# The first five microseconds of an encoder layer: early activation, ten matmuls on constants, and smaller first transfers

## The chip, the core and the metric

The kernel runs on one core of one Trainium2 chip. The metric is the device time of one execution in microseconds; lower is better. Of three runs of the kernel before, the median is 820.86 us (820.34 to 820.87). Engines are named as the profile does: PE is TensorE, DVE is VectorE, ACT is ScalarE, SP is the engine that issues most transfers; PEld are PE's weight loads. A name with q behind it (SPq, ACTq) is the queue of transfers that the engine issues.

## The reference

One layer of a bidirectional encoder trunk on 256 tokens of 1024 features, in fp32: a feed-forward half step, a mixer (latent attention beside a two-way state space scan), and a second half step. Only the beginning of the first half step matters here:

```python
def rmsnorm(x, g):
    y = xf * lax.rsqrt(jnp.mean(xf * xf, axis=-1, keepdims=True) + EPS)
    return (y * g).astype(x.dtype)

def swiglu(h, w_gate, w_up, w_down):
    return (jax.nn.silu(h @ w_gate) * (h @ w_up)) @ w_down

x = x + 0.5 * swiglu(rmsnorm(x, ffn1_norm[l]), ffn1_w_gate[l], ffn1_w_up[l], ffn1_w_down[l])
...
x = x + 0.5 * swiglu(rmsnorm(x, ffn2_norm[l]), ffn2_w_gate[l], ffn2_w_up[l], ffn2_w_down[l])
```

The hidden width of the half step is 2816, so w_gate and w_up are each 1024 x 2816.

## The kernel before

x lies transposed in SBUF, as 8 tiles (k = 0 to 7) of 128 features by 256 tokens. A half step goes through 22 blocks of 128 hidden features (f = 0 to 21). In each block PE forms the gate and the up product, [128 hidden x 256 tokens], over the 8 k tiles. To keep fp32 accuracy every operand is split in two parts of a narrower type, hi and lo: ACT writes the hi part by a copy (helper `copy`, L94) and DVE the lo part by a subtraction (helper `tt`, L97, for weights, `stt`, L100, for x). A product is then three matmuls (`mm3`, L136 to L138): hi times hi, hi weights times lo x, lo weights times hi x, the third needing the lo part of the weights. A block is therefore 2 x 8 x 3 = 48 matmuls.

A weight piece is fetched from HBM into a buffer called `raw` (4 buffers) and split into `whi` and `wlo` (4 buffers each); this is `wload`, L112. From f = 1 on a block has two pieces of 512 KB, gate and up. x is split by `Norm.scale` into `xh` and `xl` after a product with the gain, which lies in the constant tile `vec`; the sum of squares over features is collected in `nacc` (`Norm.square`), summed over features on PE (`ps_sum`, L181), turned into 1/sqrt on DVE, spread on PE (`ps_rows`, L190) and read as `R`. The products of a block leave PSUM only by a multiplication with `R`, so until `R` is there they wait in the six PSUM buffers of the tag `mm`.

In the first half step block 0 differs (L248 to L254): the weights come in four pieces of 256 KB (gate, first and second half, then up), and the eight `scale` stand between the first piece and the other three. x comes in three transfers (L166 to L168: tiles 0-1, 2-3, 4-7), the first from SP, the two others from ACT behind `vec`. PE does all 24 matmuls of gate and then all 24 of up.

Each engine runs its instructions in the order of the program; a scheduler of the language works this order out when the program is built, from priorities (`WPRI`, L31, puts the splitting of weights ahead of other work). DVE and ACT also have small work in this stretch that nothing waits for soon: rotary tables (`rp_...`), masks, and constants made from `cst` and `row`. Transfers report their end through eight counters, DMAHW0 to DMAHW7, which the program uses in turn; a transfer that gets a counter still in use by an earlier one waits in its issuing queue until that one has landed.

The name of a tile at a wait is that of the tile being written: `xh`, `xl`, `whi`, `wlo`, `ps_gu` (gate and up products).

Of the kernel before, what the change touches and what calls it, by code (L numbers as in the profile page):

```python
# [8 lines left out]
F32 = mybir.dt.float32  # L9
# [14 lines left out]
# pool depths  # L24
# [3 lines left out]
# blocks of the first half step during which the mixer's first weights are fetched  # L28
PREF = (8, 10, 12, 14, 16, 18)
# how far the splitting of weights runs ahead of other work  # L30
WPRI = 50  # L31
# emission order of the mixer, in rounds (one round per group of the state space part):
# attention units, state space units, its norm, weight chunks
# [15 lines left out]
# columns of the packed per-feature vectors  # L49
V_F1, V_MIX, V_F2, V_QA, V_KVA, V_SSM, V_DSK, V_CW, V_CB = 0, 8, 16, 24, 27, 29, 45, 61, 181  # L50
V_N = 205
# columns of the packed per-column rows
R_DTB, R_AL, R_GQ, R_GK, R_IF = 0, 64, 128, 224, 320
R_N = 336
# columns of the constant matrices
# [17 lines left out]
def build(ctx, tc, A, out, dbg=None):  # L73
# [66 lines left out]
    def wstat(ps, pieces, xh, xl, k0, first, last):  # L140
        """ps[feature, token] += sum over the k tiles held in pieces"""
        ks = [(pc, j) for pc, j0, n in pieces for j in range(j0, j0 + n)]
        for i, (pc, j) in enumerate(ks):
            mm3(ps, pc.hi[:, j * P:(j + 1) * P], pc.lo[:, j * P:(j + 1) * P],
                xh[:, k0 + i], xl[:, k0 + i], first and i == 0, last and i == len(ks) - 1)

    def rsqrt(y, v, n):
        """y = v ** -0.5 on [P, n]"""
        t = sm.tile([P, 8], I32, tag="rs_t", name="rs_t")[:, :n]
        a = sm.tile([P, 8], F32, tag="rs_a", name="rs_a")[:, :n]  # L150
        w = sm.tile([P, 8], F32, tag="rs_w", name="rs_w")[:, :n]
        ts(t, v.bitcast(I32), 1, None, ALU.logical_shift_right)
        ts(y.bitcast(I32), t, -1.0, float(0x5F3759DF), ALU.mult, ALU.add)
        ts(w, v, -0.5, None, ALU.mult)
        for _ in range(3):
            tt(a, y, y, ALU.mult)
            tt(a, a, w, ALU.mult)
            stt(y, a, 1.5, y, ALU.add, ALU.mult)

# [4 lines left out]
    x = xp.tile([P, KD, T], F32, name="x")  # L164
    nc.scalar.dma_start(vec, A["vec"])
    nc.sync.dma_start(x[:, 0:2], A["xt"][:, 0:2])  # L166
    nc.scalar.dma_start(x[:, 2:4], A["xt"][:, 2:4])
    nc.scalar.dma_start(x[:, 4:8], A["xt"][:, 4:8])  # L168
# [4 lines left out]
    V.memset(ones, 1.0)  # L173
    halfpi = cp.tile([P, 1], F32, name="halfpi")
    V.memset(halfpi, PI / 2)

    def token_sums(psp, sq, tag):
        """[token, 2]: the sum of sq[feature, token] over its features"""
        ps = psp.tile([P, 512], F32, tag=tag, name="ps_sum")
        for t in range(2):  # L180
            TE.matmul(ps[:, t:t + 1], sq[:, t * P:(t + 1) * P], ones[:, 0:1], start=True, stop=True)  # L181
        return ps[:, 0:2]

    def token_rows(psp, r, tag):
        """[P, token]: r[token, 2] on every partition"""
# [19 lines left out]
    class Norm:  # L205
        """x * gain of each tile of x as it comes, and the sum of squares"""
# [30 lines left out]
    def ffn(norm, wgu, wd, after, hook=None):  # L237
        with ExitStack() as es:
# [7 lines left out]
            for f in range(KF):  # L246
                ps = ps_mm.tile([P, 2, T], F32, tag="mm", name="ps_gu")
                if f == 0 and hook:  # L248
                    pcs = wload(wgu[f], [512], 0)
                    for k in range(KD):  # L250
                        norm.scale(k)
                    pcs += wload(wgu[f, :, 512:2048], [512] * 3, 0)
                    for j in range(2):
                        wstat(ps[:, j], [(pcs[2 * j], 0, 4), (pcs[2 * j + 1], 0, 4)], norm.xh, norm.xl, 0, True, True)  # L254
                else:
                    pcs = wload(wgu[f], [1024, 1024])
# [7 lines left out]
                tt(gu, ps, R.unsqueeze(1).to_broadcast([P, 2, T]), ALU.mult)  # L264
# [25 lines left out]
    def tables():  # L290
# [7 lines left out]
        # 0 where a pair of tokens counts, -2**100 elsewhere  # L298
# [67 lines left out]
    with ExitStack() as es:  # L366
# [63 lines left out]
        # rotated shared key and its square sum  # L430
# [12 lines left out]
        # dt = softplus(raw + bias), log-decay sums  # L443
# [22 lines left out]
        # log-decay sums counted from the middle of the sequence outwards  # L466
# [72 lines left out]
        def attn_group(g):  # L539
            st = {}  # L540

            def proj():
# [20 lines left out]
                # head norms  # L563
# [11 lines left out]
                # rotary part of q, in place  # L575
# [7 lines left out]
                # k  # L583
# [211 lines left out]
def _tiles(w):  # L795
    """[K, M] -> [M tiles, partition, K tiles, 128]"""
    k, m = w.shape
    return w.reshape(k // P, P, m // P, P).transpose(2, 1, 0, 3)


def _pairs(t):
    """[n, P, K, 128] -> [n / 2, P, 2 * K * 128]"""
# [89 lines left out]
```

## Time and profile before

| | before |
|---|---|
| median of 3 runs | 820.86 us (820.34 to 820.87) |
| profiled execution: span from first to last instruction | 817.6 us |
| PE busy | 797.8 us, 98% |
| DVE busy | 590.3 us, 72% |
| ACT busy | 470.2 us, 58% |
| read from HBM | 124.52 MB, 154 GB/s over the span |

Of the profiled execution the profile tells the span alone; the device time of a run has 3.3 us more than it (820.86 - 817.6), which lie ahead of the first instruction and behind the last. Times in rows are counted from the start of the span. A busy share of PE includes the waiting inside its pipeline, so the spacing of matmul starts says more of its pace than the share. The column PEclk reads 1.00 in all of this trace, also in the first 15 us.

### The profile page before, as it was taken

To read this page: it belongs to the slowest core of one execution; us is meant where nothing else is said; L and a number is where in the kernel's file an instruction comes from. 1 tells how busy PE (TensorE), PEld (TensorE's weight loads), DVE (VectorE), ACT (ScalarE), POOL (GpSimd) and SP (SyncE) were. 2 spreads that over 40 slices of the span, in tenths; PEclk is the share of its full clock that TensorE was granted. 3 is DMA by queue.
4 is the path that set the end of the run, shared out by engine and by line. 5 is a ranking of instruction groups with operands and counts; after the bars stand their busy time and mean duration, and the time that the engine had idled before them with its cause. 6 is when DMAs were issued, how large, how long until landed. Compare 5 with 4: busy or idle time off the path is not lost.

```text
span 817.6 us, 16082 instructions
## 1 busy us (share of the span) xinstructions
PE 797.8 (98%) x6480; PEld 768.8 (94%) x6480; DVE 590.3 (72%) x1192; ACT 470.2 (58%) x810; POOL 0.2 (0%) x4
## 2 busy tenths in 40 slices
PE   6999999999998999999999999999999999999998
PEld 5999999999998998988989999999999999999998
DVE  6977776566797986897897578657787766666543
ACT  6755554455367659679676666557455544444342
POOL 0000000000000000000000000000000000000000
PEclk9999999999999999999999999999999999999999
DMA  7667774667235443322325414342665555554772
GB/s 259 214 212 224 222 229 136 184 184 215 63 92 171 131 131 104 106 79 92 103 85 168 154 52 154 112 146 68 223 184 178 175 184 182 185 184 131 197 206 75
DMA packets 39098, 126.61 MB, mean 155 GB/s; under 512 B 4464, under 2 KB 5872, under 8 KB 39024
## 3 DMA queue, kind: packets, MB, share of 16 engines
q1 hardware_dynamic: 38592, 124.69, 48.7%
q8 instruction: 51, 0.84, 0.4%
q10 hardware_dynamic: 432, 0.89, 0.3%
q14 instruction: 23, 0.19, 0.1%
HBM read 124.52 MB, written 1.05 MB: 154 GB/s over the span
## 4 chain that ended last, share of the span: by engine, by line
PE 86%; DVE 6%; ACT 5%; DMA 2%; issue 1%; ACTq 0%
PE ps_gu L137 10%; PE ps_gu L138 10%; PE ps_gu L136 10%; PE ps_d L136 5%; PE ps_d L137 5%; PE ps_d L138 5%; PE ps_in L137 4%; PE ps_in L138 4%; PE ps_in L136 4%; PE ps_y L690 3%; PE ps_sb L138 2%; PE ps_sb L137 2%; PE ps_sb L136 2%; PE ps_sc L603 2%; PE ps_gt L137 1%; PE ps_o L630 1%
## 5 line engine op out<-in xcount | busy, mean ns | idle before, releaser
L94 ACT ACTIVATE whi<-raw 128x1024 fp32r<-128x1024 f32 (+4 forms) x256 | 251.3, 986 | 209.0 <-PE ps_d L137 53.1
L97 DVE TENSOR_TENSOR wlo<-raw,whi 128x1024 fp32r<-128x1024 f32 (+4 forms) x256 | 289.8, 1134 | 112.1 <-ACT whi L94 111.2
L136 PE MATMUL ps_gu<-xh,whi 128*128 128x256 f32 x704 | 201.0, 285 | 7.9 <-ACT whi L94 7.9
L137 PE MATMUL ps_gu<-xl,whi 128*128 128x256 f32 x704 | 201.2, 286 | 0.5 <-DVE xl L100 0.4
L138 PE MATMUL ps_gu<-xh,wlo 128*128 128x256 f32 x704 | 200.8, 285 | 0.0
L136 PEld LDWEIGHTS ps_gu<-xh,whi 128*128 128x128 f32 x704 | 136.5, 194 | 8.2 <-ACT whi L94 8.2
L137 PEld LDWEIGHTS ps_gu<-xl,whi 128*128 128x128 f32 x704 | 136.5, 194 | 1.0 <-DVE xl L100 0.9
L138 PEld LDWEIGHTS ps_gu<-xh,wlo 128*128 128x128 f32 x704 | 136.4, 194 | 0.5 <-DVE wlo L97 0.5
L137 PE MATMUL ps_in<-xl,whi 128*128 128x256 f32 x368 | 105.3, 286 | 0.1
L138 PE MATMUL ps_in<-xh,wlo 128*128 128x256 f32 x368 | 105.0, 285 | 0.0
L136 PE MATMUL ps_in<-xh,whi 128*128 128x256 f32 x368 | 104.4, 284 | 0.0
L137 PE MATMUL ps_d<-hl,whi 128*128 128x256 f32 x352 | 99.1, 281 | 0.0
L136 PE MATMUL ps_d<-hh,whi 128*128 128x256 f32 x352 | 99.1, 281 | 0.0
L138 PE MATMUL ps_d<-hh,wlo 128*128 128x256 f32 x352 | 99.0, 281 | 0.0
L137 PEld LDWEIGHTS ps_in<-xl,whi 128*128 128x128 f32 x368 | 70.1, 191 | 0.6 <-DVE xl L100 0.3
L138 PEld LDWEIGHTS ps_in<-xh,wlo 128*128 128x128 f32 x368 | 70.1, 191 | 0.5 <-issue 0.3
L136 PEld LDWEIGHTS ps_in<-xh,whi 128*128 128x128 f32 x368 | 70.1, 191 | 0.1
L136 PEld LDWEIGHTS ps_d<-hh,whi 128*128 128x128 f32 x352 | 66.3, 188 | 0.0
L137 PEld LDWEIGHTS ps_d<-hl,whi 128*128 128x128 f32 x352 | 66.3, 188 | 0.0
L138 PEld LDWEIGHTS ps_d<-hh,wlo 128*128 128x128 f32 x352 | 66.3, 188 | 0.0
L100 DVE SCALAR_TENSOR_TENSOR xz<-ps_in,vec,xz 128x254 f32<-128x254 f32 (+1 forms) x96 | 44.8, 476 | 1.6 <-ACT xz L520 0.9
L94 ACT ACTIVATE hh<-sg 128x256 fp32r<-128x256 f32 x44 | 18.1, 415 | 45.9 <-DVE sg L97 45.9
(222 smaller groups left out, 1467.5 us busy)
## 6 DMA issues: line engine op xcount, KB each, us to landing
raw<-in_w_gu SPq DMA_DIRECT2D x86, 512.0 KB, 4.5
raw<-in_w_in SPq DMA_DIRECT2D x62, 512.0 KB, 4.4
raw<-in_w_d SPq DMA_DIRECT2D x32, 384.0 KB, 3.2
raw<-in_w_d SPq DMA_DIRECT2D x32, 320.0 KB, 3.4
raw<-in_w_sb SPq DMA_DIRECT2D x16, 512.0 KB, 4.4
raw<-in_w_qkv SPq DMA_DIRECT2D x8, 544.0 KB, 3.8
raw<-in_w_ab SPq DMA_DIRECT2D x8, 512.0 KB, 3.8
raw<-in_w_o SPq DMA_DIRECT2D x8, 512.0 KB, 4.2
```

Of the source, the lines that this page charges most:

```text
L94: S.activation(dst, src, AF.Copy, scale=scale)
L97: V.tensor_tensor(out=dst, in0=a, in1=b, op=op)
L100: V.scalar_tensor_tensor(out=dst, in0=a, scalar=s, in1=b, op0=op0, op1=op1)
L136: TE.matmul(ps, whi, xhi, start=first, stop=False)
L137: TE.matmul(ps, whi, xlo, start=False, stop=False)
L138: TE.matmul(ps, wlo, xhi, start=False, stop=last)
L603: TE.matmul(sc[:, t * T:(t + 1) * T], qk[:HD, t * P:(t + 1) * P], qk[:HD, T:2 * T], start=True, stop=True)
L630: TE.matmul(po[64 * j:64 * j + 64, :T], kv[:, kt, HG * NOPE + hh_ * 64:HG * NOPE + (hh_ + 1) * 64], st[hh_][:, kt], start=kt == 0, stop=kt ...
L690: TE.matmul(py[64 * j:64 * j + 64, a:b], st[c, d][:, hh_], M[i][:, j, a:b], start=n == 0, stop=n == 3)
```

## The change

ACT gets a copy of one number, `idle`, which reads only the constant `ones`. PE gets ten fp32 matmuls of `ones` with `ones` (128 columns) ahead of everything else, into a PSUM buffer that nobody reads. x comes in four transfers of two tiles (256 KB) from SP. The weights of block 0 come in eight transfers of 128 KB: for each pair of k tiles, the gate part from ACT's queue and the up part from SP's. They go into two `raw` buffers instead of four. Block 0 is done in four steps of two k tiles: split of x and of both weight parts, then the six matmuls of gate and the six of up into two PSUM buffers instead of one, so its products are multiplied by `R` in two DVE instructions instead of one. All else is untouched (the changed file has also lost its comments, and line numbers are 4 higher in the helpers and some 33 higher further down).

```diff
+STEPS = (0, 2, 4, 6)
+NWARM = 10
...
     nc.scalar.dma_start(vec, A["vec"])
-    nc.sync.dma_start(x[:, 0:2], A["xt"][:, 0:2])
-    nc.scalar.dma_start(x[:, 2:4], A["xt"][:, 2:4])
-    nc.scalar.dma_start(x[:, 4:8], A["xt"][:, 4:8])
+    w0 = rawp.tile([P, 1088], F32, tag="raw", name="raw"), rawp.tile([P, 1088], F32, tag="raw", name="raw")
+    for i, k in enumerate(STEPS):
+        a, b = k * P, STEPS[i + 1] * P if i + 1 < len(STEPS) else DM
+        nc.sync.dma_start(x[:, a // P:b // P], A["xt"][:, a // P:b // P])
+        nc.scalar.dma_start(w0[0][:, a:b], A["w_gu1"][0, :, a:b])
+        nc.sync.dma_start(w0[1][:, a:b], A["w_gu1"][0, :, DM + a:DM + b])
...
     V.memset(ones, 1.0)
+    idle = cp.tile([P, 1], F32, name="idle")
+    S.activation(idle, ones[:, 0:1], AF.Copy)
...
+    def block0(ps_mm, ps_r, norm):
+        warm = ps_r.tile([P, 512], F32, tag="r", name="warm")
+        for _ in range(NWARM):
+            TE.matmul(warm[:, :P], ones, ones, start=True, stop=True)
+        pss = [ps_mm.tile([P, 2, T], F32, tag="mm", name="ps_gu0")[:, 0] for _ in range(2)]
+        w = [(wp.tile([P, 1088], F32R, tag="whi", name="whi"), wp.tile([P, 1088], F32R, tag="wlo", name="wlo"))
+             for _ in range(2)]
+        for i, k in enumerate(STEPS):
+            e = STEPS[i + 1] if i + 1 < len(STEPS) else KD
+            c = slice(k * P, e * P)
+            norm.scale(k)
+            for j in range(2):
+                split(w[j][0][:, c], w[j][1][:, c], w0[j][:, c])
+                if j == 0:
+                    for m in range(k + 1, e):
+                        norm.scale(m)
+            for j in range(2):
+                for m in range(k, e):
+                    s = slice(m * P, (m + 1) * P)
+                    mm3(pss[j], w[j][0][:, s], w[j][1][:, s], norm.xh[:, m], norm.xl[:, m], m == 0, m == KD - 1)
+        return pss
...
                 if f == 0 and hook:
-                    pcs = wload(wgu[f], [512], 0)
-                    for k in range(KD):
-                        norm.scale(k)
-                    pcs += wload(wgu[f, :, 512:2048], [512] * 3, 0)
-                    for j in range(2):
-                        wstat(ps[:, j], [(pcs[2 * j], 0, 4), (pcs[2 * j + 1], 0, 4)], norm.xh, norm.xl, 0, True, True)
+                    pss = block0(ps_mm, ps_r, norm)
...
+                if f == 0 and hook:
+                    for j in range(2):
+                        tt(gu[:, j], pss[j], R, ALU.mult)
```

What SP issues first, before (a row ending in x4 is four instructions; the waits in brackets are for the counters of transfers and for DVE):

```order
L166 DMA x<-in_xt 128x512
L117 DMA raw<-in_w_gu 128x512 x4
L351 DMA cst<-in_cst 128x480 [waits DMAHW0_49]
L293 DMA pos<-in_pos 128x2 [waits DMAHW1_49]
L294 DMA row<-in_row 128x336 [waits DMAHW2_49]
L117 DMA raw<-in_w_gu 128x1024 [waits DMAHW3_49,DVE_49]
```

and now:

```order
L174 DMA x<-in_xt 128x512
L176 DMA raw<-in_w_gu 128x256
L174 DMA x<-in_xt 128x512
L176 DMA raw<-in_w_gu 128x256 [waits DMAHW0_49]
L174 DMA x<-in_xt 128x512 [waits DMAHW1_49]
L176 DMA raw<-in_w_gu 128x256 [waits DMAHW2_49]
L174 DMA x<-in_xt 128x512 [waits DMAHW3_49]
L176 DMA raw<-in_w_gu 128x256 [waits DMAHW4_49]
L384 DMA cst<-in_cst 128x480 [waits DMAHW5_49]
L121 DMA raw<-in_w_gu 128x1024 [waits DMAHW6_49]
L121 DMA raw<-in_w_gu 128x1024 [waits DMAHW7_49]
```

Before, the first five transfers of SP wait for nothing. Now the first three do, and from the fourth on each waits for a counter, DMAHW0 being that of `vec` and DMAHW1 that of the first two tiles of x; `cst` and the two pieces of block 1 (the rows of 128x1024) stand behind them in the queue.

What ACT does first, before (L94 is the hi part of x or of weights):

```order
L165 DMA vec<-in_vec 128x205
L167 DMA x<-in_xt 128x512
L168 DMA x<-in_xt 128x1024
L94 ACT_TABLE_LOAD [waits DMAHW1_49]
L94 ACTIVATE xh<-x,vec 128x256 [waits DMAHW0_49]
L94 ACTIVATE whi<-raw 128x512 [waits DMAHW3_49]
L94 ACTIVATE xh<-x,vec 128x256
L94 ACTIVATE xh<-x,vec 128x256 [waits DMAHW2_49]
```

and now:

```order
L170 DMA vec<-in_vec 128x205
L175 DMA raw<-in_w_gu 128x256 x4
L183 ACT_TABLE_LOAD
L183 ACTIVATE idle<-ones 128x1 [waits DVE_49]
L98 ACTIVATE xh<-x,vec 128x256 [waits DMAHW1_49,DMAHW0_49]
L98 ACTIVATE whi<-raw 128x256 [waits DMAHW2_49]
L98 ACTIVATE xh<-x,vec 128x256
L98 ACTIVATE whi<-raw 128x256 [waits DMAHW3_49]
L98 ACTIVATE xh<-x,vec 128x256 [waits DMAHW5_49]
L98 ACTIVATE whi<-raw 128x256 [waits DMAHW4_49]
```

The load of the activation table stood behind the wait for x (DMAHW1) and now stands behind the issue of five transfers, with no wait of its own; the hi parts of x and of weights now alternate, each with the counter of its own small transfer.

What PE does first, before:

```order
L136 MATMUL ps_gu<-xh,whi 128x256 [waits Activation_49]
L137 MATMUL ps_gu<-xl,whi 128x256 [waits DVE_49]
L138 MATMUL ps_gu<-xh,wlo 128x256 [waits DVE_49]
L136 MATMUL ps_gu<-xh,whi 128x256 [waits Activation_49]
L137 MATMUL ps_gu<-xl,whi 128x256 [waits DVE_49]
L138 MATMUL ps_gu<-xh,wlo 128x256
L136 MATMUL ps_gu<-xh,whi 128x256 [waits Activation_49]
```

and now (ps_gu_139 is gate, ps_gu_140 is up):

```order
L251 MATMUL warm<-ones 128x128 [waits DVE_49]
L251 MATMUL warm<-ones 128x128 x9
L140 MATMUL ps_gu_139<-xh,whi 128x256 [waits Activation_49]
L141 MATMUL ps_gu_139<-xl,whi 128x256 [waits DVE_49]
L142 MATMUL ps_gu_139<-xh,wlo 128x256 [waits DVE_49]
L140 MATMUL ps_gu_139<-xh,whi 128x256 [waits Activation_49]
L140 MATMUL ps_gu_140<-xh,whi 128x256 [waits Activation_49]
L141 MATMUL ps_gu_140<-xl,whi 128x256
L141 MATMUL ps_gu_139<-xl,whi 128x256 [waits DVE_49]
L142 MATMUL ps_gu_139<-xh,wlo 128x256
L142 MATMUL ps_gu_140<-xh,wlo 128x256 [waits DVE_49]
```

The ten matmuls on constants wait only for DVE's memset of `ones`. Behind them gate and up share each pair of k tiles. `ps_sum` stood behind 118 matmuls of gate and up and now stands behind 149, `ps_rows` behind 154 and now behind 192; from block f = 4 on the order of PE is the same as before. On DVE, two pieces of weights instead of one are now split between `ps_sum` and `ps_rows`.

## Rows read from the trace of the kernel before

**Rows 1.** The page: busy time, share of the span and instructions of each engine.

```profile
PE 797.8 (98%) x6480; PEld 768.8 (94%) x6480; DVE 590.3 (72%) x1192; ACT 470.2 (58%) x810; POOL 0.2 (0%) x4
```

**Rows 2.** Waits of PE, whole span: engine, line <- releaser: us, times, longest.

```profile
PE ps_gu L136 <- ACT whi L94: 7.9, 2, 7.3
```

**Rows 3.** Timeline of the beginning: start us, us, engine, operation [idle before <-releaser].

```profile
0.72 0.41 ACTq L165 DMA_DIRECT2D vec<-in_vec  x1
0.73 0.39 SPq L166 DMA_DIRECT2D x<-in_xt  x1
...
4.97 1.28 ACT L94 ACT_TABLE_LOAD   x1 [4.97 <-DMA x<-in_xt]
...
6.26 0.51 ACT L94 ACTIVATE xh<-x,vec 128x256 fp32r<-128x256 f32 x1
6.68 0.61 ACT L94 ACTIVATE whi<-raw 128x512 fp32r<-128x512 f32 x1
...
7.34 0.58 PE L136 MATMUL ps_gu<-xh,whi 128*128 128x256 f32 x1 [7.34 <-ACT whi L94]
```

**Rows 4.** Timeline of PE, places between 11 and 24 us.

```profile
11.17 0.58 PE L136 MATMUL ps_gu<-xh,whi 128*128 128x256 f32 x1 [0.60 <-ACT whi L94]
...
11.89 0.58 PE L138 MATMUL ps_gu<-xh,wlo 128*128 128x256 f32 x1
...
15.05 0.41 PE L137 MATMUL ps_gu<-xl,whi 128*128 128x256 f32 x1
15.26 0.35 PE L138 MATMUL ps_gu<-xh,wlo 128*128 128x256 f32 x1
...
17.60 0.28 PE L136 MATMUL ps_gu<-xh,whi 128*128 128x256 f32 x1
...
23.36 0.28 PE L136 MATMUL ps_gu<-xh,whi 128*128 128x256 f32 x1
```

**Rows 5.** Windows: stretch, us, busy (x) of each engine, PEclk, DMA share, GB/s.

```profile
7.30:15.20 7.90, 7.26 (x29) 6.52 (x30) 7.42 (x18) 6.38 (x15) 0.00 (x0) 1.00 0.81 255
```

**Rows 6.** DMA issues at 0.7, 1.2, 19.0, 50.2 us: KB, us to landing; packets in 8:9.

```profile
vec<-in_vec ACTq DMA_DIRECT2D x1, 102.5 KB, 4.4
...
raw<-in_w_gu SPq DMA_DIRECT2D x1, 256.0 KB, 4.9
...
raw<-in_w_gu SPq DMA_DIRECT2D x1, 512.0 KB, 3.7
...
raw<-in_w_gu SPq DMA_DIRECT2D x1, 512.0 KB, 4.9
...
DMA packets 225, 0.40 MB, mean 398 GB/s; under 512 B 31, under 2 KB 61, under 8 KB 225
```

**Rows 7.** Waits of SP's queue, 0 to 30 us, columns as in the second group.

```profile
SPq L351 <- DMA vec<-in_vec: 1.8, 1, 1.8
```

**Rows 8.** Groups by form, 0 to 45 us: count | busy us, mean ns of one | idle before.

```profile
L94 ACT ACTIVATE whi<-raw 128x1024 fp32r<-128x1024 f32 x12 | 12.7, 1057 | 7.3 <-PE ps_gu L137 4.8 <-DMA raw<-in_w_gu 1.9 <-ACT sg L266 0.5
L94 ACT ACTIVATE xh<-x,vec 128x256 fp32r<-128x256 f32 x8 | 3.5, 496 | 0.4 <-DMA x<-in_xt 0.4
...
L97 DVE TENSOR_TENSOR wlo<-raw,whi 128x1024 fp32r<-128x1024 f32 x12 | 14.7, 1222 | 2.0 <-ACT whi L94 2.0
```

**Rows 9.** Timeline at 25.7 and 26.2 us: the last nacc on VectorE, ps_sum on TensorE.

```profile
25.70 0.42 DVE L97 TENSOR_TENSOR nacc<-nacc,nsq 128x256 f32<-128x256 f32 x1
...
26.18 0.61 PE L181 MATMUL ps_sum<-ones,nacc 128*128 128x1 f32 x4
```

**Rows 10.** Timeline of PE at 242 us: an fp32 operation of 128 columns.

```profile
242.06 0.49 PE L489 MATMUL ps_dup<-cst,dup 128*128 128x128 f32 x3
```

**Rows 11.** Timeline at 12.4 us (ScalarE, block 1's first piece) and 19.6 us (VectorE).

```profile
12.40 1.06 ACT L94 ACTIVATE whi<-raw 128x1024 fp32r<-128x1024 f32 x1 [0.25 <-DMA raw<-in_w_gu]
...
19.64 1.23 DVE L97 TENSOR_TENSOR wlo<-raw,whi 128x1024 fp32r<-128x1024 f32 x1 [0.23 <-ACT whi L94]
20.78 0.42 DVE L97 TENSOR_TENSOR nacc<-nacc,nsq 128x256 f32<-128x256 f32 x1
```

More of the change, by code (lines that the diff above doesn't have):

```diff
@@ L246, in ffn @@
             for f in range(KF):
-                ps = ps_mm.tile([P, 2, T], F32, tag="mm", name="ps_gu")
                 if f == 0 and hook:
-                    pcs = wload(wgu[f], [512], 0)
-                    for k in range(KD):
-                        norm.scale(k)
-                    pcs += wload(wgu[f, :, 512:2048], [512] * 3, 0)
-                    for j in range(2):
-                        wstat(ps[:, j], [(pcs[2 * j], 0, 4), (pcs[2 * j + 1], 0, 4)], norm.xh, norm.xl, 0, True, True)
-                else:
+                    pss = block0(ps_mm, ps_r, norm)
+                else:
+                    ps = ps_mm.tile([P, 2, T], F32, tag="mm", name="ps_gu")
+                    pss = ps[:, 0], ps[:, 1]
                     pcs = wload(wgu[f], [1024, 1024])
@@ L263, in ffn @@
                 gu = ev.tile([P, 2, T], F32, tag="gu", name="gu")
-                tt(gu, ps, R.unsqueeze(1).to_broadcast([P, 2, T]), ALU.mult)
+                if f == 0 and hook:
+                    for j in range(2):
+                        tt(gu[:, j], pss[j], R, ALU.mult)
+                else:
+                    tt(gu, ps, R.unsqueeze(1).to_broadcast([P, 2, T]), ALU.mult)
                 sg = ev.tile([P, T], F32, tag="sg", name="sg")
```

## The prediction

> **What bounds the kernel now.** First the busy shares of the page [rows 1]: PE has 98%, so time is saved only where PE stands still or runs slowly. Then the waits of PE over the whole span [rows 2]: its largest is for ACT's hi part of weights in the gate and up products, 7.9 us in two times, the longest 7.3. Both lie at the start of the program, so I read the timeline there. x's first transfer has landed at 4.97; only then does ACT load its table (1.28 us), and then come the hi part of x at 6.26, the hi part of weights at 6.68 and the first matmul at 7.34 [rows 3]. The second wait ends at 11.17, and the lo part makes a short one before 11.89 [rows 4].
>
> The third thing to see is PE's pace. Up to 15.26 the starts of matmuls stand 0.21 us apart (15.05 to 15.26): 256 columns at 1.2 GHz. Block 1 begins at 17.60 and block 2 at 23.36: 48 matmuls in 5.76 us, 0.12 each, the 2.4 GHz level [rows 4]. PEclk reads 1.00 in the slow stretch too [rows 5], so the spacing decides. The clock thus rose 7.9 us after the first matmul and 3.4 us after the last pause. Block 0 ends at 17.6, though its 48 matmuls are worth 5.8 us at the upper level.
>
> What counts is when block 2 can start; before that is 23.36. Behind it PE's order hardly changes and its later waits are smaller, so I carry what is gained there to the end.
>
> **The change part by part.** *Table load.* ACT issues five transfers first, of 0.41 us and a little more each [rows 3], from 0.72 to about 3, then loads the table (1.28) by 4.3, while x is on its way. `vec` lands at 0.72 + 4.4 = 5.1 [rows 3, 6]. The first weights share the second place in the queues; before, 256 KB in that place landed at 1.17 + 4.9 = 6.1 [rows 6]. Hi parts of 256 columns take up to 0.5 [rows 8], so the first matmul starts at 6.5 instead of 7.34.
>
> *Ten matmuls.* They are not in this trace. The nearest row is a 128-column fp32 operation at the upper level, three in 0.49 us, starts 0.11 apart [rows 10]; a matmul of fp32 numbers may take two of these (the two of `ps_sum` stand as four in their row, [rows 9]), so ten cost 1.1 (one each) to 4.4 us (two each, at half the clock) and run from 1.0 to 5.4 at the latest. They are hidden by PE's wait to 6.5; without that cover they would cost those 1.1 to 4.4. What they can give is the upper clock at 6.5.
>
> *Held transfers.* SP's fourth transfer (up, second step) needs the counter of `vec`, and so is issued at 5.1; `cst` showed this wait of 1.8 us in the kernel before [rows 7]. Everything behind it on SP is held as well: in order u1, x2, u2, x3, u3 (up parts and x pieces of the steps, counted from 0), then `cst`, then block 1. Their latency stands in no row, so I bound it: 512 KB on a queue without others took 3.7 to 4.9 us [rows 6], of which 1.3 is moving at 398 GB/s, leaving 2.4 to 3.6; I take 3.0. u1 lands at 5.1 + 0.3 + 3.0 = 8.4. The others follow at 398 GB/s: x2 9.1, u2 9.4, x3 10.1, u3 10.4, `cst` 11.1, and block 1's gate at 12.4.
>
> The Trainium skill speaks against this edit: "DMA: Bandwidth & Descriptors", section "Rules for kernel authors", wants a megabyte or more in a transfer and small ones merged. The trace has 398 GB/s in a microsecond of 256 KB transfers [rows 6], so at that size no loss is seen; 128 KB pieces no row shows. By the rule, the late landing below would be the result.
>
> *Block 0.* A step costs ACT four parts of 0.4 to 0.5 us [rows 8] and DVE four of 0.42 at most (the 256-column `nacc`, [rows 9]): some 1.8 us a step. PE's twelve matmuls cost 1.4 at the upper level and 2.6 at the lower one. With x3 at 10.1, ACT is done at 11.9, DVE at 12.3, PE at 12.9.
>
> *Block 1.* Its gate lands at 12.4, which is when it was taken up before too [rows 11]. Hi 1.06, lo 1.22 [rows 8]: the third matmul, which needs the lo part, starts at 14.8. 46 more at 0.12 end block 1 at 20.3. Before: 23.36. Gain 3.0.
>
> This wait is what takes the place of the old ones, and it sets how little the clock is worth: were PE still at the lower level until 13, it would have done 30 matmuls by then and end block 0 at 15.2, and block 2 would start at 20.9.
>
> *Sum of squares.* `ps_sum` now stands behind 149 matmuls, so PE comes there at 20.3 + 53 x 0.12 = 26.7. DVE then needs, from 14.8 on, six pieces (1.14 from start to start, [rows 11]), seven `nacc` at 0.34 and about 2.2 us of small work: 11.4, so 26.2 to 26.5. Before it was 26.1 [rows 9]. DVE is thus just in time and no more. Between `ps_sum` and `ps_rows` DVE has one more piece (1.14), PE seven more matmuls (0.84): 0.3 us lost. With 0.1 for the rest, the gain is 2.6.
>
> Two PSUM buffers instead of one for block 0, two multiplications of 256 instead of one of 512 columns and the copy of one number lie beside matmuls and are set at nothing; if DVE were late after `R`, each could cost a further instruction's 0.1.
>
> **The sum.** 817.6 of span less 2.6 is 815.0; the 3.3 us around it, taken from the median of the runs (the profile gives the profiled execution's span alone), make 818.3.
>
> **The rivals.**
>
> *Early landing.* The held transfers take 2.4 instead of 3.0, and `ps_rows` does not wait: gain 3.6, 817.3. For it: two rows of 512 KB at both ends of this latency. Against: queues are full here.
>
> *Late landing.* 1.69 MB lie from u1 to block 1's gate. At 398 GB/s they take 4.2 us; at the 255 GB/s that the same stretch had before [rows 5] 6.6, so the gate lands at 14.8, its lo part is there at 17.1 and block 2 starts at 22.6: gain 0.8, less 0.4: 820.4, no change. For it: eight transfers of rows half as long, five of them held. Against: in the old stretch the queue also waited for buffers, which it does not here.
>
> *The matmuls on constants do not do what they are for.* The clock rises at 15.3 as before. PE has then done 41 matmuls, ends block 0 at 16.2, and block 2 starts at 21.9: gain 1.4, less 0.1: 819.5. For it: the matmuls between 7.34 and the pause before 11.17 did not raise it. Against: ten make a longer unbroken run, and block 0 has no pause at the lower level.
>
> The Trainium skill ("TensorE: Matmul & The Clock Gate", "What's actually happening") says that the lower clock is the resting state and that matmul activity ends it. The trace agrees in the rise at 15.26; by that rule any matmul counts, also one of constants, and this rival falls.
>
> *The clock stays low.* Gate and up by turns wait for ACT and DVE in every step, and PE pauses until block 1's lo part at 14.8. If the clock then takes the 7.9 us of the old start, it rises at 22.7. From 6.5 on at 0.21, PE reaches 76 matmuls; before it had these done at 17.6 + 28 x 0.12 = 21.0. That is 1.7 slower: 822.6. From a rise at 18.7 on it is a loss. For it: the pauses of the rows kept the clock down. Against: at the lower level PE needs 2.6 us a step and its supply 1.8, so it would not pause, and then the clock rises.
>
> **Chances.** Forecast 0.50 (817.7 to 819.0), early landing 0.13, late landing 0.19, clock as before 0.10, clock low 0.08. A measurement of this kernel can tell 0.2%, 1.64 us, from no change, so faster means under 819.2: forecast 0.49, early 0.13 and 0.03 of the clock as before give 0.65. Slower: clock low and 0.01 of the late landing, 0.09. Same: 0.26. The range goes from the early landing with 0.3 to spare, 817.0, to the late one with 0.2, 820.6.
>
> **What the profile after would show.** The table load ends before 5, the first `ps_gu` starts near 6.5, spaced 0.12 if the clock is up. SP's fourth transfer waits for `vec`. Block 1's third matmul waits for DVE's lo part near 14.8; block 2 starts at 20.3 where it was 23.36. `ps_sum` stays near 26.5, with more matmuls ahead of it. Wrong would be: block 1's gate landing after 14, spacing of 0.21 past 13, a wait at `ps_sum` of over 0.5, or a gain in block 2 that is gone at the end.

## The result, and the profile after

The changed kernel takes 821.8 us (median of 12 runs, 819.7 to 823.04), the kernel before 820.22 (12 runs, 819.26 to 822.58): a ratio of 1.0020, 95% interval 1.0012 to 1.0029. It is slower by 0.2%; 818.3 was forecast. The profiled execution took 820.29 us with a span of 818.5, so 1.8 us lie around the span.

The page's busy row, the waits of PE over the whole span, and its mean granted clock, to be held against [rows 1, 2]:

```profile
PE 801.7 (98%) x6500; PEld 772.4 (94%) x6500; DVE 590.7 (72%) x1197; ACT 470.8 (58%) x815; POOL 0.2 (0%) x4
```

```profile
PE ps_gu L140 <- ACT whi L98: 3.0, 3, 1.9
...
PE ps_in L140 <- DVE x L104: 0.9, 1, 0.9
PE ps_gu L142 <- DVE wlo L101: 0.8, 1, 0.8
```

```profile
core 0: 818.5 us, clock 0.998
```

The waits of 7.9 us at the start have shrunk to 3.0, and yet nothing is gained. A wait for `ps_in`, which the kernel before did not have, is new. The beginning, to compare with [rows 3]:

```profile
1.04 4.63 PE L251 MATMUL warm<-ones 128*128 128x128 f32 x20 [1.04 <-DVE ones L181]
...
3.09 1.28 ACT L183 ACT_TABLE_LOAD   x1 [3.09 <-issue]
...
4.93 0.33 SPq L176 DMA_DIRECT2D raw<-in_w_gu  x1
4.94 0.51 ACT L98 ACTIVATE xh<-x,vec 128x256 fp32r<-128x256 f32 x1 [0.35 <-DMA vec<-in_vec]
...
6.01 0.56 PE L140 MATMUL ps_gu<-xh,whi 128*128 128x256 f32 x1 [0.33 <-ACT whi L98]
```

This part did what it was meant to: the table load is off the path, the ten matmuls (20 records) end at 5.7, and the first `ps_gu` starts at 6.01 instead of 7.34. Then PE's timeline, beside [rows 4]:

```profile
10.32 0.39 PE L140 MATMUL ps_gu<-xh,whi 128*128 128x256 f32 x1 [0.78 <-ACT whi L98]
...
13.53 0.28 PE L142 MATMUL ps_gu<-xh,wlo 128*128 128x256 f32 x1
15.70 0.39 PE L140 MATMUL ps_gu<-xh,whi 128*128 128x256 f32 x1 [1.89 <-ACT whi L98]
15.92 0.28 PE L141 MATMUL ps_gu<-xl,whi 128*128 128x256 f32 x1
16.95 0.58 PE L142 MATMUL ps_gu<-xh,wlo 128*128 128x256 f32 x1 [0.76 <-DVE wlo L101]
...
19.68 0.41 PE L142 MATMUL ps_gu<-xh,wlo 128*128 128x256 f32 x1
19.90 0.37 PE L140 MATMUL ps_gu<-xh,whi 128*128 128x256 f32 x1
...
23.93 0.28 PE L140 MATMUL ps_gu<-xh,whi 128*128 128x256 f32 x1
```

Block 0 ends at 13.8 where it ended at 17.8: 4 us are won. Block 1's first hi part comes only at 15.70, its first lo part at 16.95, and from there to 19.9 the starts stand 0.21 apart again. Block 2 begins at 23.93, 0.57 later than before. The windows of that trace (stretch, length, busy time and count of PE, PEld, DVE, ACT, POOL, PEclk, DMA share, GB/s; the first is the stretch of [rows 5]) show the clock at half from 17 to 20 us, the 1.2 GHz level:

```profile
7.30:15.20 7.90, 5.73 (x42) 5.11 (x40) 5.14 (x17) 4.44 (x12) 0.00 (x0) 1.00 0.83 288
8.00:10.00 2.00, 1.55 (x12) 1.31 (x11) 0.74 (x3) 0.82 (x3) 0.00 (x0) 1.00 0.75 244
10.00:12.00 2.00, 1.68 (x11) 1.50 (x12) 2.00 (x6) 2.00 (x7) 0.00 (x0) 1.00 0.74 228
17.00:20.00 3.00, 3.00 (x14) 3.00 (x15) 2.90 (x10) 2.50 (x5) 0.00 (x0) 0.50 0.76 258
20.40:23.90 3.50, 3.50 (x31) 3.50 (x31) 3.00 (x7) 1.79 (x3) 0.00 (x0) 1.00 0.73 252
```

Why block 1 came late is in the transfers. SP's wait (to [rows 7]), then x's third piece (issued 5.30) and block 1's gate (issued 7.68), and the packets moved in three of the microseconds, from 5, 8 and 10 us on (to [rows 6]):

```profile
SPq L176 <- DMA vec<-in_vec: 2.9, 1, 2.9
```

```profile
x<-in_xt SPq DMA_DIRECT2D x1, 256.0 KB, 4.1
...
raw<-in_w_gu SPq DMA_DIRECT2D x1, 512.0 KB, 6.9
...
DMA packets 348, 0.36 MB, mean 362 GB/s; under 512 B 43, under 2 KB 300, under 8 KB 348
...
DMA packets 189, 0.28 MB, mean 277 GB/s; under 512 B 20, under 2 KB 88, under 8 KB 189
...
DMA packets 118, 0.21 MB, mean 206 GB/s; under 512 B 13, under 2 KB 102, under 8 KB 118
```

x's third piece landed at 9.4, block 1's gate at 14.6. Of the transfers between them, up's last part landed at 11.3 (forecast 10.4) and `cst` at 13.3 (forecast 11.1). Between 10 and 11 us 102 of 118 packets are under 2 KB and the rate is half of the 398 GB/s of [rows 6]. Rows of 1 KB alone do not explain that: from 5 to 6 us, while the transfers issued at the start are moving, 300 of 348 packets are under 2 KB and the rate is 362. From 8 to 12 us the DMA engines are busy for three quarters of the time only (0.75 and 0.74 in the windows above).

Further on come the sums, to be held against [rows 9], and the first `ps_in` of the mixer:

```profile
30.02 0.43 DVE L101 TENSOR_TENSOR nacc<-nacc,nsq 128x256 f32<-128x256 f32 x1
...
30.50 0.60 PE L191 MATMUL ps_sum<-ones,nacc 128*128 128x1 f32 x4
...
203.30 0.28 PE L142 MATMUL ps_d<-hh,wlo 128*128 128x256 f32 x1
204.47 0.39 PE L140 MATMUL ps_in<-xh,whi 128*128 128x256 f32 x1 [0.90 <-DVE x L104]
```

The last `nacc` is at 30.02 and `ps_sum` at 30.50, some 4 us later than forecast; PE loses no more than 0.2 us there, since block 2 came late too.

The offset to the kernel before, matmul by matmul: 0.57 us late at block 2; 0.85 from block 5 on, since `ps_rows` waits 0.2 for `diag`; 1.06 more at the first `ps_in`, of which 0.17 has come back by 222 us, so that the matmuls are 1.74 late there; and 0.71 back at 257 us, where the wait for `ps_cb` had been 0.9 and is 0.2. Small drifts leave 0.93 at the end, the 0.9 by which the spans differ (818.5 and 817.6).

The medians differ by more. The mean granted clock of a run tells of that: one of the 12 runs of the changed kernel has 1.000 (819.7 us), the others 0.998 or 0.996 (820.3 to 822.3 us) and one 0.993 (823.0). Of the kernel before, 25 of the 29 runs that stand beside the first four experiments have 1.000. The mean counts the stretch ahead of the first rise as 1.00 (PEclk reads 1.00 there), so it tells of falls alone. The profiled run has 0.998 and one fall; seven of the 12 runs have less, so in them the clock was low for longer. Where, no trace shows.

### The profile page after: what moved, and what is told of

Its sections match the earlier page's. It is cut to its first block, busy times and chain, and to the rows that moved or that the text cites. A ratio compares the mean times of both kernels' runs of the same rounds, so it can differ in the third digit from the quotient of the medians.

```text
span 818.5 us, 16140 instructions
## 1 busy us (share of the span) xinstructions
PE 801.7 (98%) x6500; PEld 772.4 (94%) x6500; DVE 590.7 (72%) x1197; ACT 470.8 (58%) x815; POOL 0.2 (0%) x4
## 4 chain that ended last, share of the span: by engine, by line
PE 86%; DVE 6%; ACT 5%; DMA 1%; issue 1%; SPq 0%; ACTq 0%; DVEq 0%
PE ps_gu L142 10%; PE ps_gu L141 10%; PE ps_gu L140 10%; PE ps_d L141 5%; PE ps_d L140 5%; PE ps_d L142 5%; PE ps_in L141 4%; PE ps_in L142 4%; PE ps_in L140 4%; PE ps_y L723 3%; PE ps_sb L142 2%; PE ps_sb L141 2%; PE ps_sb L140 2%; PE ps_sc L636 2%; DVE wlo L101 1%; PE ps_gt L141 1%
```

## The experiments

Twelve kernels, each timed in turns with the kernel before on the same chip; ratios are to it, and its median in each set is named where it is first used. "Offset" is how much earlier (+) or later (-) a matmul starts than the same one in [rows 4] or its trace.

**e1, without the matmuls on constants.**

```diff
-NWARM = 10
+NWARM = 0
```

> The changed kernel without the ten matmuls on constants, all else as changed. Theory A (the held transfers bring block 1's gate late, at 14.6 instead of 12.4, and the long pause that this gives PE lets the clock fall): the supply does not depend on the ten matmuls, so the gate lands at 14 to 15 and the third matmul of block 1 starts near 17 again, but PE, still at 0.21 us a matmul, is busy until it and the clock has no reason to fall: block 2 starts near 22.5, 0.9 us before its 23.36 of before, some 1.5 us faster than the changed kernel. Rival B (the ten matmuls save what they were put there for and the loss is only the late gate): without them block 0 ends 2 us later and the kernel is as slow as the changed one or slower.

820.39 us, before 819.7, ratio 1.0010 (1.0001 to 1.0018). The clock rose at 11.0, block 0's last matmul started at 14.55 (13.53 with them), block 1 at 16.17, the clock fell at 17.8 as well, block 2 at 24.54. The ten matmuls do raise the clock and save 1 us in block 0; by block 2 0.6 is left, and the median without them is no higher. What comes after block 0 decides.

**e2, the pause before block 1 filled.**

```diff
+NFILL = 17
...
+        fill = ps_r.tile([P, 512], F32, tag="r", name="fill")
+        for _ in range(NFILL):
+            TE.matmul(fill[:, :T], w[1][1][:, DM - P:DM], norm.xl[:, KD - 1], start=True, stop=True)
```

> The changed kernel with 17 more matmuls (2.0 us at the upper level) on block 0's last operands behind block 0, into a buffer that nobody reads, so that PE is busy while it waits for block 1's gate. Theory A: the gate still lands near 14.6 and the third matmul of block 1 starts near 17, but the clock does not fall (spacing 0.12 from 17 to 20), so block 2 starts at 22.5 instead of 23.9: 1.4 us faster than the changed kernel at least, 0.9 faster than before. If the clock falls for another reason than the pause, nothing is won and up to 0.3 lost.

The clock did not fall at 17, and block 2 began at 22.41, 1.5 us earlier than in the changed kernel. But 823.09 us (6 runs), ratio 1.0043 (1.0026 to 1.0059). Its waits of PE from 14 to 45 us, and windows at 17, 30.5 and 262.5:

```profile
PE ps_sum L192 <- DVE nacc L102: 1.3, 1, 1.3
```

```profile
17.00:20.00 3.00, 3.00 (x26) 3.00 (x26) 2.90 (x10) 2.59 (x5) 0.00 (x0) 1.00 0.65 214
...
30.50:33.50 3.00, 3.00 (x16) 3.00 (x16) 2.83 (x19) 0.14 (x1) 0.00 (x0) 0.50 0.44 156
...
262.50:265.70 3.20, 3.20 (x16) 3.20 (x17) 2.72 (x8) 3.18 (x7) 0.00 (x0) 0.50 0.00 1
```

So the fall at 17 goes with the pause: it is gone here, and the three other kernels that keep the pause and these transfers (e1, e5, e10) have it too, between 17.0 and 17.8. The 1.5 us did not last: PE came to `ps_sum` before DVE's sums were there, waited, and the clock fell behind that wait, and once more at 262 us. The second limit was the sums.

**e3, eight transfers instead of thirteen, none held.**

```diff
-STEPS = (0, 2, 4, 6)
+STEPS = (0, 4)
...
+    nc.sync.dma_start(x[:, 0:2], A["xt"][:, 0:2])
+    nc.scalar.dma_start(w0[0][:, 0:512], A["w_gu1"][0, :, 0:512])
+    nc.sync.dma_start(w0[1][:, 0:512], A["w_gu1"][0, :, DM:DM + 512])
+    nc.scalar.dma_start(x[:, 2:4], A["xt"][:, 2:4])
+    nc.sync.dma_start(x[:, 4:8], A["xt"][:, 4:8])
...
```

> The changed kernel with the first transfers cut so that they are eight in all and none waits for a counter: vec, x in three (two, two and four tiles), block 0's weights in four of 256 KB; two steps of four k tiles; ten matmuls and early activation kept. Theory A: with nothing held, cst and block 1's gate follow at once, the gate lands by 12.5, the third matmul of block 1 starts by 14.9, block 2 by 20.5: 2.5 to 3 us faster than before. Rival C (the queues are simply slow in this stretch, held or not): the gate lands at 14 to 15 again and block 2 does not start before 22.5.

820.47 us, ratio 1.0014 (1.0004 to 1.0024). Block 1's gate landed at 11.6 (14.6 in the changed kernel), so the late supply is of the transfers' making. But the ten matmuls ended at 5.25, the first `ps_gu` started at 6.85, and the clock fell at 8.1; x's tiles 2-3 landed only at 8.64, behind 256 KB of gate in the same queue. Windows of this run:

```profile
5.30:8.00 2.70, 0.93 (x5) 0.62 (x5) 1.57 (x3) 1.20 (x3) 0.00 (x0) 1.00 1.01 357
8.10:14.80 6.70, 6.19 (x26) 5.66 (x27) 5.56 (x13) 6.13 (x12) 0.00 (x0) 0.50 0.88 332
```

Block 2 began at 22.77, offset +0.6, and it was lost at `ps_sum` (a wait of 0.9). Four of the 12 runs show no fall of the clock (mean 1.000) and still take 819.6 to 820.3 us.

**e4, the kernel before with the activation and the ten matmuls alone.**

```diff
+    idle = cp.tile([P, 1], F32, name="idle")
+    S.activation(idle, ones[:, 0:1], AF.Copy)
...
+                    for _ in range(10):
+                        TE.matmul(warm[:, :P], ones, ones, start=True, stop=True)
```

> The kernel before with the early activation and the ten matmuls alone; transfers and order of block 0 as before. Theory A: first matmul near 6.1 instead of 7.34, the upper clock from about 6.4, block 1's gate at 12.3 as before, block 2 at 20.5 if the clock stays up (2.8 faster than before) and about 23 if a pause before block 1 brings it down (0.3 faster). Rival: as slow as the changed kernel, 0.5 us behind before at block 2; then the transfers are not the cause.

820.19 us, ratio 1.0013 (1.0002 to 1.0024). The clock rose at 4.0, fell at 7.5 and rose again only at 17.7, 2.3 us later than before; block 2 at 24.87. Here an early rise with a pause behind it (1.82 us up to the first `ps_gu` at 6.78) was worse than none. A block 2 behind that of before was the rival's sign, but its conclusion does not hold: the fall at 7.5 lies within block 0, where the changed kernel has none, so e4 says nothing of the transfers. e3 does.

**e5, the ten matmuls write to a buffer of the six.**

```diff
-        warm = ps_r.tile([P, 512], F32, tag="r", name="warm")
+        warm = ps_mm.tile([P, 2, T], F32, tag="mm", name="warm")
```

> The changed kernel with one edit: the ten matmuls write to a buffer of the pool of six PSUM buffers (ps_mm) and no longer to one of the pool ps_r. The order of instructions on every engine stays as it is. Theory A (rotation of buffers): in the kernel before, the first feed forward takes 1 + 21 + 8 = 30 of the six buffers in turn, so the last ps_d stands in buffer 5 and the mixer's first ps_in, which takes the place of buffer 0, needs nothing that is late; in the changed kernel block 0 takes two buffers, 31 in all, the last ps_d stands in buffer 0, and the first ps_in at 202 us waits 0.9 us for DVE's read of it. With one buffer more (32) the last ps_d stands in buffer 1: that wait goes, the loss of 1.06 us at this matmul with it, of which 0.4 comes back within 20 us anyway, so 0.6 us of the time goes: 821.2 against 821.8 of the changed kernel on the same scale, ratio to before near 1.0012. Theory B (the wait comes of the start being 0.85 us late, by a changed meeting of engines or transfers): the wait stays at 0.9 us and the time at 821.8.

The order of every engine is that of the changed kernel. PE at the same place as in the last rows of the changed kernel:

```profile
203.21 0.28 PE L142 MATMUL ps_d<-hh,wlo 128*128 128x256 f32 x1
203.33 0.28 PE L140 MATMUL ps_in<-xh,whi 128*128 128x256 f32 x1
```

No wait; the last matmul's offset is -0.23 where it was -0.93. The rotation of the six PSUM buffers made it: block 0 takes two of them instead of one, and with 31 in turn the last `ps_d` stands in the buffer that the mixer's first `ps_in` needs. The other runs agree: each kernel with 31 (the changed one, e1, e2, e3, e9) has the wait of 0.9, and none with 30 or 32 has it. In the median this is not told apart (821.13, before 819.62, ratio 1.0018, 1.0008 to 1.0028), because falls of the clock (none of 12 runs at 1.000) spread the times over 5 us.

**e6, the kernel before with the activation alone.** The edit is the first pair of lines of e4.

> The kernel before with the activation on a constant alone, without the ten matmuls and with the transfers as they were. Theory A (the table load is worth little here, since the first block is paced by TensorE at 1.2 GHz and by x's second half): first ps_gu at 6.6 where it was 7.3, block 1 at 17.2 where it was 17.6, the clock up at about the same time, block 2 between 22.9 and 23.4, the sums of squares at the same place: 819.5 to 820.2 where before has 819.9, no difference that can be told. If so, what e4 lost at block 2 (1.5 us) was the ten matmuls' doing. Theory B (the activation shifts ScalarE's order against SyncE's and costs as much as it gives, so that e4's loss came from it): block 2 at 24.5 or later and 820.5 or more.

819.38 us, ratio 0.9998 (0.9989 to 1.0006), 10 of 11 runs at 1.000. First `ps_gu` at 6.92, block 2 at 23.73 (23.36 before), last matmul at +0.07. Worth nothing and harmless: e4's loss was the matmuls'.

**e7, x first, none held, matmuls on constants up to the data.** The edit to e3; the edit of e5 is in it too.

```diff
-NWARM = 10
+NWARM = 16
...
-    nc.sync.dma_start(w0[1][:, 0:512], A["w_gu1"][0, :, DM:DM + 512])
-    nc.scalar.dma_start(x[:, 2:4], A["xt"][:, 2:4])
+    nc.sync.dma_start(x[:, 2:4], A["xt"][:, 2:4])
+    nc.scalar.dma_start(w0[1][:, 0:512], A["w_gu1"][0, :, DM:DM + 512])
```

> All that the runs so far point to in one kernel: eight transfers of 2 to 4 KB a row, none of them held; x goes in one queue ahead of everything (k tiles 0-1, 2-3, 4-7), gate and up of block 0 in two halves in the other; 16 matmuls on constants, so that TensorE goes on until the first data; these write to a buffer of ps_mm. Theory A (the supply of block 0 and the falls of the clock after pauses are what the changed kernel lost): first ps_gu at 6.7, clock up at 4.7 and not down before block 2, block 0 done by 13.3, block 1 behind it at once, block 2 near 19.3 (23.36 before), ps_sum near 26.5 behind DVE's nacc with a wait of 1 to 2 us, no wait at the first ps_in: 817 to 818.5 where before has 819.9. Rival B (DVE's chain up to nacc sets the start whatever TensorE does): ps_sum not before 28.5, a wait of 3 us there and the clock down behind it: 819.5 to 821. Rival C (the clock falls within block 0 all the same): block 2 at 22.5 or later, 820 to 821.

Up to block 2 as theory A had it: clock up at 4.6, block 0's last matmul at 14.23, block 2 at 20.14, offset +3.2. Then `ps_sum` in PE's timeline, two waits of DVE on the way to it, and the clock in the windows:

```profile
28.02 0.38 PE L193 MATMUL ps_sum<-ones,nacc 128*128 128x1 f32 x2 [2.09 <-DVE nacc L101]
```

```profile
16.82 1.23 DVE L101 TENSOR_TENSOR wlo<-raw,whi 128x1024 fp32r<-128x1024 f32 x1 [0.89 <-ACT whi L98]
...
21.07 1.23 DVE L101 TENSOR_TENSOR wlo<-raw,whi 128x1024 fp32r<-128x1024 f32 x1 [0.94 <-ACT whi L98]
```

```profile
14.20:28.00 13.80, 11.73 (x98) 11.53 (x96) 11.77 (x29) 9.31 (x16) 0.00 (x0) 1.00 0.79 269
28.50:31.80 3.30, 3.30 (x17) 3.30 (x17) 3.06 (x20) 0.82 (x3) 0.00 (x0) 0.50 0.47 161
```

From block 1's first lo part (done at 14.5) to the end of the last `nacc` (28.0) DVE took 13.5 us, 1.8 of them waiting for hi parts of weights in these two places. At block 5 the offset is -0.13: all of it gone, B's mechanism behind A's start. 820.57 us, ratio 1.0012 (1.0000 to 1.0025); 818.2 in the one run at 1.000.

**e8, e7 with a second buffer for the squares.** ACT's next square then need not wait for DVE to add the one before, and the scheduler puts `ps_sum` 24 matmuls earlier.

```diff
-                sq = sm.tile([P, T], F32, tag="nsq", name="nsq", bufs=1)
+                odd = self.vcol == V_F1 and self.n % 2
+                sq = sm.tile([P, T], F32, tag="nsq1" if odd else "nsq", name="nsq", bufs=1)
```

> e7 with a second buffer for the squares of the first norm (nsq and nsq1 by turns), so that ScalarE's next square need not wait for VectorE's sum of the one before; the scheduler then puts the last nacc and ps_sum 24 matmuls earlier. Theory A (what ate e7's 3.2 us at block 2 was VectorE's chain of sums, which ended at 27.9, with the fall of the clock behind the wait of 2.1 us for it): last nacc near 23, ps_sum there with a wait under 1 us, no fall of the clock at 28; the offset of some 2 to 3 us is carried to the end of the first feed forward, 817.5 to 818.5 where before has 819.6, more runs at a mean clock of 1.0. Rival B (the supply of weights, 512 KB in 4.5 us from issue to landing behind each buffer set free, holds TensorE at the pace of before whatever the sums do): the sums come early, but TensorE then waits for whi in blocks 3 to 6, and blocks from the fifth on stand within 0.5 us of before: 819.5 to 820.5.

818.79 us, before 819.81, ratio 0.9985 (0.9972 to 0.9998): faster. In the profiled run `ps_sum` starts at 24.75, still with a wait of 1.9 us, and the clock holds (the window of e7's fall):

```profile
28.50:31.80 3.30, 3.29 (x26) 3.04 (x25) 3.30 (x12) 2.44 (x3) 0.00 (x0) 1.00 0.52 165
```

Offset +1.5 at block 5 and +2.1 at the end. Six of 12 runs are at 1.000 (816.4 to 818.6), the rest 818.9 to 820.8: the sums came 3 us earlier, not 5 as expected, and half the runs still show a fall of the clock. No trace says where.

**e9, e8 without matmuls on constants** (NWARM = 0).

> e8 without the matmuls on constants. Theory A (these matmuls raise the clock before the data is there, and their gain in block 0 is small beside what every later pause of 1 to 2 us can cost at a raised clock): first ps_gu at 6.9, TensorE at 1.2 GHz until some 10 to 15 us, block 0 done near 15, no wait for block 1's weights since they land at 12, block 2 near 20.9 to 21.7, no fall of the clock after it, most runs at a mean clock of 1.0: 817.8 to 818.6, as fast as e8 or faster. Rival B (the early clock is what brings the gain): block 2 at 22.5 or later and 819 or more, slower than e8 by 1 us.

820.13 us, ratio 1.0003 (0.9992 to 1.0014). Clock up at 13.3, block 2 at 21.52 as in A, yet 0.4 is left at block 5. With no matmul to write it, `warm` takes no buffer, 31 are in turn again, and the wait of 0.9 at `ps_in` is back: the rotation a second time. `ps_sum` has also moved, behind 103 matmuls instead of 119, with a wait of 1.4. Neither theory's time can be read from it cleanly.

**e10, the changed kernel with the edits of e5 and e8 alone, and e11, the kernel before with the activation and the second buffer for squares.**

> The changed kernel with the two last edits of e8 alone: the ten matmuls write to a buffer of ps_mm (as in e5) and the squares of the first norm take two buffers by turns. Transfers, steps and the number of matmuls on constants stay as in the changed kernel; ps_sum stands 24 matmuls earlier than there. Theory A (the transfers are what costs the changed kernel its start, and the sums matter only once the data is early): block 1's gate lands at 14.5 and the clock falls at 17 as in the changed kernel, block 2 at 23.9, ps_sum near 27 with a wait of 0 to 1.5 us, no wait at the first ps_in: 820.5 to 821.3, slower than before by 1 us. Rival B (the sums alone were what ate the gain): 819 or less, and most of e8's gain over before without its transfers.

> The kernel before with the activation on a constant (as in e6) and two buffers by turns for the squares of the first norm; transfers as in the kernel before, no matmul on constants. The scheduler puts ps_sum 25 matmuls earlier (behind 93). Theory A (TensorE at 1.2 GHz paces the start of this kernel, and its sums came just in time): block 2 at 23.7 as in e6, ps_sum near 24 with a wait of 1 to 2 us for nacc, the rest as before: 819.3 to 820.5, no better than before. Rival B (the sums bound the kernel before too): ps_sum without a wait, and 818.5 or less.

e10: 821.38 us, before 819.53, ratio 1.0021 (1.0009 to 1.0032); block 1 at 15.69, block 2 at 24.06, clock down from 17.6 to 21.0. e11: 819.43, ratio 1.0002 (0.9993 to 1.0010), all 11 runs at 1.000, block 2 at 24.16; `ps_sum` at 23.30 without a wait, as rival B had it, and yet A's time. The sums bind only once the data is early; without e7's transfers the second buffer gives nothing.

**e12, e8 with the second halves held.** Three transfers of 512 bytes take three counters; x's second half, the second halves of gate and up and all behind them wait for `vec`, in large pieces. Gate's second half also moves from ACT's queue to SP's.

```diff
+    for i in range(3):
+        tiny = cp.tile([P, 1], F32, name="tiny%d" % i)
+        nc.sync.dma_start(tiny, A["vec"][:, i:i + 1])
     nc.sync.dma_start(x[:, 4:8], A["xt"][:, 4:8])
-    nc.scalar.dma_start(w0[0][:, 512:DM], A["w_gu1"][0, :, 512:DM])
+    nc.sync.dma_start(w0[0][:, 512:DM], A["w_gu1"][0, :, 512:DM])
```

> e8 with three transfers of 512 bytes ahead of x's second half, which take three of the eight counters: x's second half, gate's and up's second halves and all behind them on SyncE are then held for the counter of vec, as five of the transfers of the changed kernel are, but with their size as in e8 (512, 256 and 256 KB, 2 to 4 KB a row). ps_sum comes 26 matmuls earlier in the order than in e8. It tells apart the two reasons for the late landing of block 1's gate in the changed kernel (14.55, against 11.45 in e8). Theory A (the size of the pieces: rows of 1 KB, at 206 to 291 GB/s): held at 5.0, x's second half lands at 8.5 to 9.2 (8.15 in e8), gate's at 10 (9.2 in e8), block 1's gate near 12.5 at some 390 GB/s, and block 2 within 1 us of e8's 19.9. Theory B (the hold itself: queues that restart give some 250 GB/s whatever the size): x's second half at 9.5 or later, block 1's gate at 14 or later, block 2 at 22 or later.

x's second half (issued 4.96) and block 1's gate (issued 7.02) among the transfers, then the windows with PEclk, DMA share and GB/s at the end:

```profile
x<-in_xt SPq DMA_DIRECT2D x1, 512.0 KB, 4.5
...
raw<-in_w_gu SPq DMA_DIRECT2D x1, 512.0 KB, 6.0
```

```profile
6.00:8.00 2.00, 1.52 (x11) 1.02 (x9) 1.16 (x3) 1.82 (x5) 0.00 (x0) 1.00 0.97 249
8.00:10.00 2.00, 2.00 (x16) 1.93 (x16) 1.32 (x3) 1.31 (x5) 0.00 (x0) 1.00 0.93 272
10.00:12.00 2.00, 1.59 (x11) 1.19 (x11) 1.90 (x5) 2.00 (x6) 0.00 (x0) 1.00 0.98 366
```

The gate landed at 13.0: 11.45 in e8, 14.55 in the changed kernel. Of the 3.1 us, 1.6 come with the hold (and with what else the edit does: the three small transfers, and one queue for all), 1.5 are left for the size and number of the held pieces. Held queues move 249 to 272 GB/s from 6 to 10 us with the DMA engines busy 0.93 to 0.97 (389 and 412 GB/s in e8), and large pieces are back at 366 from 10 on, where the changed kernel's small ones had 228. That all of it goes through one queue is not the reason, since SP's queue, alone at work, moved 426 GB/s in e8 from 10 to 11 us. The two losses also differ in kind: in the changed kernel the engines were busy 0.74 from 10 to 12 us, here 0.98. What left them idle there stays open. Neither theory alone. Block 2 is at 22.76, but PE has waited for `ps_sum` ahead of it here, so that does not speak for B.

And this kernel has the lowest ratio: 817.50 us (816.51 to 818.38), before 819.46, ratio 0.9973 (0.9963 to 0.9983). The interval overlaps that of e8, so the two are not told apart. ACT, waiting for the held half, took the first square at 8.4 instead of 13.8, and the sums came earlier: `ps_sum` at 21.86, ahead of block 2 now, with a wait of 0.9 us. Block 5 is at 40.76 (40.50 in e8) and the last matmul at +1.3 (+2.1 in e8), but 7 of 9 runs are at 1.000, against 6 of 12. So what speaks for this kernel is fewer falls of the clock, not an earlier start. That the shorter wait for the sums is why the clock holds is not shown: it fits e7 (2.1 us, 1 run of 12 at 1.000), e8 (1.9, 6 of 12) and e12 (0.9, 7 of 9), but not e9 (1.4, 5 of 12).

## Why the prediction was wrong, step by step

*Table load and matmuls on constants:* right. First `ps_gu` 6.01 for 6.5, clock up at 6.4; the rival that they would not raise it fell. The ten ended at 5.7, a little behind the bound of 5.4.

*Held transfers: the step that failed.* SP's wait for `vec` came as forecast (issue at 4.93 for 5.1), and the latency was right (up's second part 7.8 for 8.4, x's third piece 9.4 for 9.1). "The others follow at 398 GB/s" was wrong: from there to block 1's gate took 5.1 us, not 3.3. The rate came from a stretch of full queues with rows mostly of 2 KB [rows 6]; here the transfers were held and small, and moved 244 and 228 GB/s from 8 to 12 us. Of their delay against e8, about half comes with the hold (e12). The other half goes with small held pieces; their rows of 1 KB alone are not the cause (362 GB/s from 5 to 6 us), and why the DMA engines stood idle a quarter of the time stays open. The late-landing rival had this, from the 255 GB/s of [rows 5]: gate at 14.8, lo part at 17.1 (14.55 and 16.95 measured). That it came so close is partly luck, as its rate was that of other pieces, in a stretch where the queue also waited for buffers. It had 0.19; the row of the same stretch should have weighed more than the best microsecond.

On this point the Trainium skill, "DMA: Bandwidth & Descriptors", section "Rules for kernel authors", asks for few large transfers. The trace agrees in the direction: 228 GB/s from 10 to 12 us in the changed kernel, 366 with larger pieces in e12.

*Block 0 and 1:* block 0 ended at 13.8 for 12.9. Block 1's lo part was 2.15 late; the pause it caused brought the clock down, and 14 matmuls at 0.21 instead of 0.12 cost another 1.3. Together these are 3.45 of the 3.6 by which block 2 missed 20.3. I had the clock fall or stay low only as a failure to rise. That a pause *after* the rise takes the clock away stood in no term.

The Trainium skill, "TensorE: Matmul & The Clock Gate", section "HAM oscillation — how this bites in real kernels", describes waits for DMA between groups of matmuls that throttle the clock again. The trace agrees in that, with 0.50 from 17 to 20 behind waits of 1.89 and 0.76 us; e2 without that pause kept 1.00. It differs in their length: the waits that the page describes are of some 3 to 5 us.

*Sum of squares: a second term of the wrong size.* I gave DVE 11.4 us from block 1's first lo part to the last `nacc`. It took 13.5, in the changed kernel (16.9 to 30.45) as in e7 (14.5 to 28.0); the sum had no term for DVE's waits for hi parts, 1.8 us in e7. The late block 2 hid this in the changed kernel. Had block 2 come at 20.3, PE would have waited at `ps_sum`: in e7, with block 2 at 20.14, it waited 2.09 us, the clock fell behind it, and all of the 3.2 us was lost. So the forecast of 818.3 would probably have failed here too. The forecast 0.3 at `ps_rows` was a wait of 0.2.

*Two PSUM buffers at nothing:* wrong by 0.70 at the end (-0.93 against -0.23 in e5), lost 180 us later. I looked for cost where the edit stands, not at who takes that buffer next.

*Base:* I put 3.3 us around the span; the profiled executions have 1.8. On that base the same gain of 2.6 would have read 816.8. The profiled execution of the kernel before was thus one of the faster ones (819.4 by this base, where the 12 runs have a median of 820.22).

*Carried to the end:* the order behind block 4 is the same, but the offset changed at two places (-0.89 at `ps_in`, +0.71 at `ps_cb`), and most runs lost the clock for longer than the profiled one.

## What to carry to other kernels

Work out what a faster start runs into next, one bound at a time: here the first data, then block 1's weights, then DVE's sums, each of which took the gain of the one before as long as it was left (the changed kernel, e2, e7), and the kernels that were faster had moved all three (e8, e12). TensorE's clock brought up early gained 1 us in block 0 (e1) and 1.6 by block 2 (e8 against e9), but it was lost again where a pause followed (e4, e3), since a wait can cost the clock on top of the wait. An edit that takes one more buffer from a rotating pool is to be followed to the pool's next user.

## What the runs showed of the hardware

- The clock came down behind waits of 1.89 and 0.76 us (changed kernel, 0.50 from 17 to 20 us), 1.3 (e2) and 2.09 (e7). Behind waits of 1.9 (e8), 1.4 (e9) and 0.9 (e12) it held in the profiled run, so the length alone does not decide. The runs of one kernel also differ: in e8 six of 12 have a mean clock of 1.000, the others 0.998 or 0.996.
- A matmul of 128 fp32 columns on constants is two records: 20 for ten.
- With the held transfers of 256 to 512 KB (e12), 249 and 272 GB/s moved from 6 to 8 and 8 to 10 us with the DMA engines busy 0.97 and 0.93; in e8 the same stretches had 389 and 412 GB/s. So a busy share near one does not mean full rate.
- Rows of 1 KB were not slow by themselves: with 300 of 348 packets under 2 KB, 362 GB/s moved from 5 to 6 us of the changed kernel, and 206 from 10 to 11 us, where the transfers had been held.
